# Gated-delta layer of a two-layer trunk: one decay matrix per unit, query products scaled after TensorE, the state's product set apart, the later modulation begun at the sixth unit

## The chip, the cores and the metric

The kernel runs on one core of one Trainium2 chip. Its engines work side by side and meet through semaphores: TensorE (PE in the profile, its weight loads PEld), VectorE (DVE), ScalarE (ACT), GpSimd (POOL) and the queue that starts the DMAs (SP). The metric is the time on the device of one execution, in microseconds (us). The kernel before takes 2041.61 us (median of 3 executions, 2041.05 to 2041.88).

## What is computed

Two layers on 1024 tokens of width 1024, all in float32. Layer A is a gated DeltaNet mixer, layer B a softmax attention with forget gates; only layer A is touched. In each layer the input is normalised and modulated by a shift, a scale and a gate that come from a conditioning vector (`cond @ ada_w[i]`). For layer A, per head and per chunk of tokens:

```python
g = jnp.cumsum(g, axis=-1)
decay = jnp.exp(jnp.where(lower, g[..., :, None] - g[..., None, :], -jnp.inf))
L = jnp.where(strict, jnp.einsum('bhncd,bhnsd->bhncs', kb, k) * decay, 0.0)
T = lax.linalg.triangular_solve(eye + L, ...)
u = T @ vb
w = T @ (kb * jnp.exp(g)[..., None])
attn = jnp.einsum('bhncd,bhnsd->bhncs', q, k) * decay
def step(state, inp):
    v_new = u_n - jnp.einsum('bhcd,bhde->bhce', w_n, state)
    o = (jnp.einsum('bhcd,bhde->bhce', q_n, state)
         + jnp.einsum('bhcs,bhse->bhce', a_n, v_new))
    state = state * gl_n[..., None, None] + jnp.einsum('bhcd,bhce->bhde', k_n, v_new)
    return state, o
```

Here q, k are normalised to length one, `kb`, `vb` are k and v times beta, `q_n` is q times exp(g), `k_n` is k times exp(g_last - g). There are 8 query/key heads and 16 value heads, so each key head serves two value heads.

## The kernel before

**Units.** Layer A is cut into 16 units: the sequence in two halves of 512 tokens (h = 0, 1), and in each half the 8 key heads (g = 0 to 7) with two value heads j each. The kernel uses chunks of 128 tokens (the result doesn't depend on the chunk), so a unit has 4 chunks. For each unit TensorE projects k, q, two times v and two gates z (`proj_tile`): 8 contraction steps of three matmuls with 512 columns each (high and low parts of the operands), evicted by `proj_conv` through ACT, three DVE steps of the short convolution and a tanh.

**A unit's steps**, each a Python generator:

- `decay` (L852) broadcasts the cumulated gates from DRAM into `gb` (128 x 1024), POOL masks it with an affine select (L861), and ACT takes exp with a bias, one instruction per head and chunk (L873). It runs twice a unit: `d1` (strictly lower, tokens on the partitions) for L, and `d2` (upper with diagonal, transposed) for attn.
- `prepk` (L878) brings k into token layout (`to_tokens`: 4 transposes, the squares on ACT, a copy to `ktok`, L919 and L923), forms 1/|k| with POOL's power (L888), the factors `un`, `wn`, `weg`, and L itself (`lm`) on DVE from the product k k^T in PSUM.
- `invert_blocks` inverts the 16 x 16 diagonal blocks: `lm`'s blocks go through DRAM into `lr` (one block per partition), 15 pairs of small DVE instructions (L1086, L1090) do the elimination, and the result comes back through DRAM into `r` (`rmat<-rb`). `invert_merge` then joins blocks to 32, 64 and 128 with small matmuls in banks "su" and "tr"; four DVE transposes (L1113) make `tm`, the transposed blocks, which its second group of matmuls needs.
- `prepv` (L926) brings q's squares and v into token layout (`vtok`, one copy of 128 x 512 per head, L923) and lets POOL scale v by `un` (L939, four instructions).
- `prep2` (L942) runs `decay` for d2, takes exp of `gb` on ACT (L949), multiplies q with it on POOL for each of the two heads (`qd`, L950), and forms `am` = (k q^T) times d2 on DVE (L958).
- `chain` (L962) is the recurrence, four chunks in order. Per chunk: PE k times state into bank "ch" (128 x 256); DVE `xp` (L978); PE r times `xp`; ACT copies it to `vn` (L991) and DVE scales it to `ve` (L992); then into bank "co", for each head, PE `qd` times state and `am` times `vn` accumulated, and at once `ktok` times `ve` (128 x 256); DVE updates the state (L1011); ACT takes the squares for the output norm and copies the output to `og` (L1017, L1020). Banks "ch" and "co" are single.
- `finish` (L1031) scales `og`, transposes it, multiplies with the z gate, splits it into high and low part (`ogh` on ACT, `ogl` on DVE) for both heads, and stores both with two DMAs of 512 KB.

**Other work.** `next_norm` normalises the second half's tokens during the first units. `ada_all` forms the later modulation (the gate of layer A, all of layer B) in 16 strips of 256 columns: 8 loads of 128 KB (`oraw`), 8 DVE instructions (L272, L274), a product with a vector of ones on PE, an eviction (L301) from a bank of the projections. It starts when the first gates are there. `out_proj_a` follows the projections.

**What sets the order.** PE's instructions stand in the order in which they are recorded. `Flow` keeps a list of generators with priorities and a clock of estimated PE time; each `yield n` makes its generator due n ns later, the first due one in priority order goes next, and the projections (priority 9) fill the rest. The numbers `Y_...` are such delays (how long a step waits for other engines' work before its next matmul is recorded), the numbers `R_...` say how long after the recording of an eviction its PSUM bank counts as free. They are estimates: if an engine is later than its number, PE waits, since it takes its instructions in order. The other engines' orders come from a scheduler with priorities; they too are fixed when the kernel is built, and each engine waits at its head instruction.

Of the kernel before, what the change touches and what calls it, by code (L numbers as in the profile page):

```python
# [8 lines left out]
F32 = mybir.dt.float32  # L9
F32R = mybir.dt.float32r  # L10
# [27 lines left out]
Y_PK = 1200  # L38
# [4 lines left out]
Y_P2 = 4000  # L43
# [8 lines left out]
Y_C2 = 2000  # L52
Y_F0 = 9000
Y_F1 = 800
Y_F2 = 2550
# [30 lines left out]
ADP = 2000  # L86
R_AD = 600
R_OA = 1150
# [95 lines left out]
def tile_trunk(  # L184
# [74 lines left out]
    def ada_strip(alloc, palloc, layer, col, width, wtag, atag, btag, ahead, pace):  # L259
# [38 lines left out]
        else:  # L298
# [3 lines left out]
            flow.free(ps, R_AD)  # L302
# [207 lines left out]
    with ExitStack() as sa:  # L510
# [34 lines left out]
        def start_norm():  # L545
            xsT = [at([P, HALF], n, b) for n, b in (("k", KQ), ("k", KQ), ("k", KQ), ("q", 2), ("q", 2))]
            xsT += [at([P, HALF], "ktok", 3) for _ in range(3)]
            for t in range(CPH):
                xt = at([P, D], *(("vtok", 3), ("qd", 2))[t // 2])
                nc.sync.dma_start(xt, x[t * P : (t + 1) * P, :])  # L550
                for d in norm_tile(xt, at([P, D], "ogt", 1), lambda k, p, t=t: nc.scalar.copy(
                    xsT[k][:, t * P : (t + 1) * P], p)):
                    flow.t += d
# [11 lines left out]
            for n in range(2):  # L565
                ps = banks[n]
                acc = at([P, D], "d2", 2)
# [43 lines left out]
        def norm_tile(xt, jk, evac):  # L611
            rs = rms_rows(xt, jk, at)
# [13 lines left out]
        def next_norm():  # L626
            yield from hold(lambda: done["kqv"] >= 2)
            for t in range(CPH):
                tok = CPH * P + t * P
                xt = at([P, D], "nx", 1)  # L630
                if t == 0:
                    nc.vector.tensor_copy(xt[:, 0:KT], ts[0]["gt"]["ngc"][:, 0, 0:KT])
                nc.sync.dma_start(xt, x[tok : tok + P, :])
                yield 4000
                hf = at([P, KT, P], "nh", 1)

                def evac(k, p):
                    nc.vector.tensor_scalar(
                        hf[:, k], p, gcol[0][:, k : k + 1], scol[0][:, k : k + 1],
                        op0=ALU.mult, op1=ALU.add,  # L640
                    )

                yield from norm_tile(xt, hf.rearrange("p k t -> p (k t)"), evac)
                yield 3000
                nc.sync.dma_start(
                    h1_d[:, :, t * P : (t + 1) * P].rearrange("k p t -> p k t"), hf
                )
# [12 lines left out]
        def gates(h, gt):  # L660
# [44 lines left out]
            nc.scalar.activation(ex, ex, AF.Exp)  # L705
            ngc = at([P, CPH, 16], "g_ngc", 2)
# [12 lines left out]
            gt.update(col=col, ex=ex, ngc=ngc, beta=beta, g_d=g_d)  # L719
# [54 lines left out]
        def proj_all():  # L774
            for i in range(2 * NG):
# [21 lines left out]
                yield from hold(lambda: done["prep2"] >= i - 1)  # L797
                t["q"] = qf = at([P, CPH, P], "q", 2)
# [53 lines left out]
        def decay(t, name):  # L852
# [6 lines left out]
            dv = at([P, 2 * CPH, P], name, 2)  # L859
            low = name == "d1"  # L860
            nc.gpsimd.affine_select(  # L861
                out=dv, in_=gb.rearrange("p j (c t) -> p (j c) t", t=P),
                compare_op=ALU.is_gt if low else ALU.is_ge, fill=BIG if low else -BIG, base=0,
                pattern=[[0, 2 * CPH], [-1 if low else 1, P]], channel_multiplier=1 if low else -1,
            )
            bias = t["gt"]["col" if low else "ngc"]
            yield Y_DG
            for j in range(2):
                for c in range(CPH):
# [4 lines left out]
                        dv[:, u], dv[:, u], AF.Exp, scale=-1.0 if low else 1.0, bias=bias[:, c, hd : hd + 1]  # L874
                    )
            return gb, dv

        def prepk(t):  # L878
            g, gt, kf = t["g"], t["gt"], t["k"]
            _, d1v = yield from decay(t, "d1")  # L880
            yield Y_PK
            t["ktok"] = ktok = at([P, CPH, P], "ktok", 3)
            t["ss"] = ss = at([P, 2, CPH], "gss", 3)
# [3 lines left out]
            nc.vector.tensor_scalar(rk, ss[:, 0], EPS, None, op0=ALU.add)  # L887
            nc.gpsimd.tensor_tensor(rk, rk, mhalf[:, 0:CPH], op=ALU.pow)  # L888
            rkb = bc(rk, 2, 2)
            t["un"] = un = at([P, CPH, 2], "un", 3)  # L890
            t["wn"] = wn = at([P, CPH, 2], "wn", 2)
            t["weg"] = weg = at([P, CPH, 2], "weg", 3)
# [967 lines left out]
```

## Time and profile before

| | us |
|---|---|
| median of 3 executions | 2041.61 |
| the profiled execution's own time | 2033.73 |
| its span | 2032.0 |
| PE busy in the span | 1846.4 |
| first to last projection matmul of layer A | about 45 to 1035 |
| output projection of layer A | about 1036 to 1281 |
| layer B | about 1281 to 2023 |

The profile is of one execution. A "wait" of PE is time in which PE had nothing running, put down to what released it. Two things are needed to read the PE rows. A matmul of plain float32 is two records, one of the split high/low type is one. And a record's length is modelled and overlaps the next record, so what a matmul costs is read from start to start, not from its length. The granted clock (PEclk) is 1.0 at full speed and 0.5 when throttled.

### The profile page before, as it was taken

The page shows a single profiled execution, that of the slowest core. Times are in us where ns is not written, and L with a number is a line of the kernel's source. Part 1 is how long each engine was busy: PE and PEld are TensorE (multiplying, and loading weights), DVE is VectorE, ACT ScalarE, POOL GpSimd, SP SyncE. Part 2 cuts the span into 40 slices and gives each one's busy share as a digit, 9 for nine tenths or more (in the row PEclk, how much of TensorE's full clock was granted, in tenths as well). Part 3 has the DMA queues.
Part 4 walks back from the last instruction along what each step waited for, and adds up shares of the span by engine and source line. Part 5 has one row for each costly group of instructions (what it writes and reads, how often), then busy time and mean ns, then how long its engine had stood idle before and what let it go on. Part 6 is the DMA issues. An engine that isn't in the chain of part 4 may idle for free. (4 is left out here: it accounts for less than half of the span.)

```text
span 2032.0 us, 36238 instructions
## 1 busy us (share of the span) xinstructions
PE 1846.4 (91%) x12940; PEld 1539.1 (76%) x12940; DVE 1375.5 (68%) x3319; ACT 1035.2 (51%) x2684; POOL 483.0 (24%) x518
## 2 busy tenths in 40 slices
PE   4878899998998989999989789999999999999898
PEld 3766677777776777777777567789889889889676
DVE  5788888787878566766656467456666666656764
ACT  4555466555545445555444344255655655655631
POOL 2140232221213021222101223331231231331222
PEclk6999899999999999999999899999999999999999
DMA  6686676766656455454469988020110220211523
GB/s 248 229 258 226 219 240 208 227 214 223 187 173 172 127 160 160 155 163 134 134 225 311 328 299 285 23 64 22 63 63 17 68 63 16 65 56 42 167 85 96
DMA packets 235781, 315.72 MB, mean 155 GB/s; under 512 B 103176, under 2 KB 155936, under 8 KB 235600
## 3 DMA queue, kind: packets, MB, share of 16 engines
q1 hardware_dynamic: 235600, 313.41, 47.6%
q8 instruction: 102, 1.67, 0.3%
q14 instruction: 79, 0.65, 0.1%
HBM read 231.67 MB, written 81.67 MB: 154 GB/s over the span
## 5 line engine op out<-in xcount | busy, mean ns | idle before, releaser
L129 PE MATMUL mm<-ht_h,whi 128*128 128x512 f32 x784 | 352.4, 450 | 7.2 <-DVE olo L301 5.6
L129 PE MATMUL mm<-ht_l,whi 128*128 128x512 f32 x784 | 317.5, 405 | 3.9 <-DVE ht_l L601 3.9
L129 PE MATMUL mm<-ht_h,wlo 128*128 128x512 f32 x784 | 318.0, 406 | 1.8 <-POOL wlo L328 1.8
L129 PE MATMUL mm<-whi,h_h 128*128 128x384 f32 x512 | 187.0, 365 | 0.9 <-DVE kn L1449 0.9
L129 PEld LDWEIGHTS mm<-ht_h,whi 128*128 128x128 f32 x784 | 154.6, 197 | 40.1 <-DVE olo L301 6.5
L129 PEld LDWEIGHTS mm<-ht_h,wlo 128*128 128x128 f32 x784 | 153.4, 196 | 37.8 <-POOL wlo L328 2.2
L129 PEld LDWEIGHTS mm<-ht_l,whi 128*128 128x128 f32 x784 | 155.0, 198 | 31.0 <-DVE ht_l L601 5.2
L764 DVE SCALAR_TENSOR_TENSOR cv_y<-cv_t,conv_h,cv_y 128x512 f32<-128x512 f32 x192 | 147.6, 769 | 43.0 <-ACT cv_y L756 40.8
L129 PE MATMUL mm<-whi,h_l 128*128 128x384 f32 x512 | 173.0, 338 | 0.0
L129 PE MATMUL mm<-wlo,h_h 128*128 128x384 f32 x512 | 172.7, 337 | 0.0
L1600 DVE TENSOR_TENSOR ptl<-pt,pth 128x512 fp32r<-128x512 f32 x192 | 106.3, 555 | 93.9 <-ACT pth L1599 92.2
L1599 ACT CAST pth<-pt 128x512 fp32r<-128x512 f32 x192 | 91.1, 476 | 140.0 <-PE pt L133 139.2
L1443 POOL TENSOR_TENSOR rs<-ss,mhalf 128x4 f32<-128x4 f32 x64 | 64.5, 1007 | 332.4 <-DVE ss L1441 326.7
L328 DVE TENSOR_TENSOR wlo<-ht_h,whi 128x512 fp32r<-128x512 f32 x124 | 91.1, 775 | 59.7 <-ACT whi L325 54.7
L1564 ACT ACTIVATE lg<-lg,mx 128x896 f32<-128x896 f32 (+7 forms) x128 | 99.5, 777 | 55.4 <-DVE mx L1556 49.7
L325 ACT CAST whi<-ht_h 128x512 fp32r<-128x512 f32 x124 | 70.7, 618 | 95.8 <-PE mm L129 35.3
L129 PE MATMUL mm<-h_h,whi 128*128 128x512 f32 x240 | 99.9, 416 | 0.7 <-DVE wlo L1699 0.3
L129 PEld LDWEIGHTS mm<-whi,h_h 128*128 128x128 f32 x512 | 97.8, 191 | 3.5 <-ACT v L1445 1.2
L129 PEld LDWEIGHTS mm<-wlo,h_h 128*128 128x128 f32 x512 | 97.4, 190 | 2.0
L133 PE MATMUL pt<-ident,lg 128*128 128x128 f32 (+1 forms) x584 | 95.6, 272 | 2.4 <-ACT lg L1564 2.4
L325 ACT CAST whi<-wlo 128x512 fp32r<-128x512 f32 (+1 forms) x108 | 62.5, 625 | 67.2 <-DMA wlo<-in_wa_c_dram 30.9
L129 PEld LDWEIGHTS mm<-whi,h_l 128*128 128x128 f32 x512 | 96.6, 189 | 0.0
(366 smaller groups left out, 4702.0 us busy)
## 6 DMA issues: line engine op xcount, KB each, us to landing
ht_h<-in_wa_o_dram SPq DMA_DIRECT2D x62, 512.0 KB
wc<-whi SPq DMA_DIRECT2D x45, 512.0 KB
wc<-wlo SPq DMA_DIRECT2D x45, 512.0 KB
wlo<-wc SPq DMA_DIRECT2D x45, 512.0 KB
whi<-wc SPq DMA_DIRECT2D x45, 512.0 KB
wlo<-in_wa_c_dram SPq DMA_DIRECT2D x35, 512.0 KB
oraw<-in_ada_w_dram SPq DMA_DIRECT2D x128, 128.0 KB
gb<-g_d SPq DMA_DIRECT2D x32, 512.0 KB
```

The costliest lines, as they stand in the source:

```text
L129: self.nc.tensor.matmul(out, lhsT, rhs, start=start, stop=stop)
L133: self.nc.tensor.transpose(out, src, ident)
L325: nc.scalar.copy(hi, src)
L328: (lo_eng or nc.gpsimd).tensor_tensor(lo, src, hi.bitcast(F32), op=ALU.subtract)
L764: nc.vector.scalar_tensor_tensor(y, raw[:, j : j + HALF], w[:, j : j + 1], y, op0=ALU.mult, op1=ALU.add)
L1443: nc.gpsimd.tensor_tensor(rs, ss, mhalf[:, 0:4], op=ALU.pow)
L1564: nc.scalar.activation(lg, lg, AF.Exp, scale=-1.0, bias=mx[:, hh : hh + 1], accum_out=sums[:, tt : tt + 1],)
L1599: nc.scalar.copy(ph_[:, cs], pp[:, cs])
L1600: nc.vector.tensor_tensor(pl_[:, cs], pp[:, cs], ph_[:, cs].bitcast(F32), op=ALU.subtract)
```

## The change

It touches layer A alone.

- **One decay matrix.** `d1` is no longer computed. `lm` is built from `d2`, so it holds the transposed L; the inversion's elimination and the merging matmuls are rewritten for that (operands swapped, same counts). The first group of the merging matmuls now reads the transposed blocks `tm`. A unit has one load of `gb`, one affine select and 8 exps in place of two, two and 16.
- **Scalings moved.** v is scaled by |k| while ACT takes it out of PSUM (two instructions of 128 x 256 per bank), where before POOL multiplied it. `vn` is scaled by beta/|k|^2 while ACT takes it out (two of 128 x 128 in place of one of 128 x 256). exp of `gb` on ACT and `qd` on POOL are gone.
- **Query product.** In place of `qd` times state in bank "co" per head, one product q times state (128 x 256) goes into bank "ch" right behind r times `xp`; ACT takes it out scaled by exp(g), two instructions (`qe`, L1023); DVE adds it to the output on the way out of "co" (`og`); the squares are then taken from `og`.
- **The state's product apart.** Between `am` times `vn` and `ktok` times `ve` stands a delay `Y_C3` = 1000. Other delays: `Y_C2` 2000 to 1700, `Y_PK` 1200 to 1000, `Y_P2` 4000 to 3000; bank "ch" counts as free 1000 ns later.
- **Later modulation.** `ada_all` starts when the sixth unit's k is recorded, and the bank of a gate strip counts as free 2500 instead of 600 ns after its eviction (`R_AS`).
- **Smaller ones.** q has three buffers; `next_norm` loads ahead into two buffers and stores by half tiles; `finish` works head by head with `ogt`, `ogh`, `ogl` of one head, single buffers, and four stores of 256 KB.

```diff
-Y_P2 = 4000
+Y_P2 = 3000
...
-Y_C2 = 2000
+Y_C2 = 1700
+Y_C3 = 1000
...
+AD0 = 5
 R_AD = 600
+R_AS = 2500
...
-            flow.free(ps, R_AD)
+            flow.free(ps, R_AS)
...
-                yield from hold(lambda: done["prep2"] >= i - 1)
-                t["q"] = qf = at([P, CPH, P], "q", 2)
+                t["q"] = qf = at([P, CPH, P], "q", KQ)
...
         def prepk(t):
-            _, d1v = yield from decay(t, "d1")
+            t["d2"] = yield from decay(t)
...
                     nc.vector.scalar_tensor_tensor(
-                        d1v[:, u], mq[:, c * P : (c + 1) * P], wn[:, c, j : j + 1], d1v[:, u],
+                        lm[:, u], mq[:, c * P : (c + 1) * P], wn[:, c, j : j + 1], t["d2"][:, u],
...
+                    nc.scalar.activation(
+                        vtok[:, c].rearrange("p j f -> p (j f)"), tr[:, o : o + 2 * P], AF.Copy,
+                        scale=t["irk"][:, c : c + 1],
+                    )
...
-            for c in range(CPH):
-                nc.gpsimd.tensor_tensor(vtok[:, c], vtok[:, c], bc(t["un"][:, c], 2, P), op=ALU.mult)
...
-            gb, d2 = yield from decay(t, "d2")
...
-                nc.scalar.activation(gb[:, j], gb[:, j], AF.Exp)
-                nc.gpsimd.tensor_tensor(
-                    qd[:, j], qf, gb[:, j].rearrange("p (c t) -> p c t", t=P), op=ALU.mult
-                )
...
-                nc.scalar.copy(vn, p1[:, 256:512])
+                for j in range(2):
+                    nc.scalar.activation(
+                        vn[:, j * P : (j + 1) * P], p1[:, 256 + j * P : 256 + (j + 1) * P], AF.Copy,
+                        scale=wn[:, c, j : j + 1],
+                    )
...
-                flow.free(p1, R_C)
+                if not first:
+                    mm(p1[:, 0:256], qf[:, c], st)
+                    qe = at([P, 2 * P], "qe", 2)
+                    for j in range(2):
+                        sl = slice(j * P, (j + 1) * P)
+                        nc.scalar.activation(
+                            qe[:, sl], p1[:, sl], AF.Copy, scale=ex[:, 1, c, 2 * g + j : 2 * g + j + 1]
+                        )
+                flow.free(p1, R_C + 1000)
                 yield Y_C1
                 p2 = yield from pst("co", 1)
                 for j in range(2):
                     sl = slice(j * P, (j + 1) * P)
-                    if not first:
-                        mm(p2[:, sl], qd[:, j, c], st[:, sl], start=True, stop=False)
-                    mm(p2[:, sl], am[:, j, c], vn[:, sl], start=first, stop=True)
+                    mm(p2[:, sl], am[:, j, c], vn[:, sl])
+                yield Y_C3
                 mm(p2[:, 256:512], ktok[:, c], ve.rearrange("p j f -> p (j f)"))
...
+                    nc.vector.tensor_tensor(oc, p2[:, 0:256], qe, op=ALU.add)
...
-                nc.scalar.copy(og[:, c].rearrange("p j f -> p (j f)"), p2[:, 0:256])
...
+                ogt = at([P, HALF], "ogt", 1)
...
+                ogh, ogl = at([P, HALF], "ogh", 1, F32R), at([P, HALF], "ogl", 1, F32R)
+                split(ogh, ogl, ogt, lo_eng=nc.vector)
+                yield Y_F2
+                for v, d in ((ogh, og_d), (ogl, ogl_d)):
+                    nc.sync.dma_start(d[2 * g + j, :, h * HALF : (h + 1) * HALF], v.bitcast(F32))
...
-                        pbk[b][o : o + 16, us], lm[sls[b], u, o : o + 16], r[sls[b], u, o + 16 : o + 32],
+                    mm(pbk[b][sls[b], us], lm[h16, u, sls[b]], tms[b][0:16, u, 0:16], start=True, stop=True)
...
         def ada_all():
-            yield from hold(lambda: done["gates"] == 1)
+            yield from hold(lambda: done["kp"] >= AD0 + 1)
```

Three places show how the instructions move. First ACT's order before, at the first unit: `sqt` are the squares of transposed k (L919), d_731 is the first unit's `d1`, `ktok` and `vtok` the copies that free PSUM bank "tr".

```order
L919 ACTIVATE sqt,gss<-tr 128x128
L873 ACTIVATE d_731<-d_731,g_gc 128x128 x8
L919 ACTIVATE sqt,gss<-tr 128x128 x3
L923 COPY ktok<-tr 128x512
L768 ACTIVATE cv_t<-cv_y 128x512
L919 ACTIVATE sqt,gss<-tr 128x128 x2
L923 COPY vtok<-tr 128x4x128
```

ACT's order now, at the same place (d_734 is the one decay matrix `d2`):

```order
L935 ACTIVATE sqt,gss<-tr 128x128 x4
L939 COPY ktok<-tr 128x512
L935 ACTIVATE sqt,gss<-tr 128x128 x4
L787 ACTIVATE cv_t<-cv_y 128x512
L889 ACTIVATE d_734<-d_734,g_ngc 128x128 x8
L956 ACTIVATE vtok<-tr,irk 128x256 x4
```

The eight exps have moved from ahead of three of k's squares and the `ktok` copy to behind them and behind q's squares.

Second PE's order before, in one chunk of the chain of the second unit (state_140 is its state, d_1214 its `am`, mm the projections that fill):

```order
L133 MATMUL tr<-ident,og 128x128 x4
L129 MATMUL co<-state_140,qd 128x128
L129 MATMUL co<-vn,d_1214 128x128
L129 MATMUL co<-state_140,qd 128x128
L129 MATMUL co<-vn,d_1214 128x128
L129 MATMUL co<-ve,ktok 128x256
```

PE's order now, in the same chunk:

```order
L132 MATMUL ch<-xp,rmat_129 128x128 x2
L132 MATMUL ch<-state_140,q 128x256
L136 MATMUL tr<-ident,og 128x128 x4
...
L132 MATMUL co<-vn,d_832 128x128 x2
L132 MATMUL mm<-ht_h,whi 128x512
L132 MATMUL mm<-ht_l,whi 128x512
L132 MATMUL mm<-ht_h,wlo 128x512
L132 MATMUL mm<-ht_h,whi 128x512
L132 MATMUL mm<-ht_l,whi 128x512
L132 MATMUL mm<-ht_h,wlo 128x512
L136 MATMUL tr<-ident,og 128x128 x4
L132 MATMUL co<-ve,ktok 128x256
```

The product with `ve` stood directly behind the ones with `vn`; now six projection matmuls stand between. Of the 64 chunks 36 have six there, 18 have three and 10 none; before, none had any.

Third ACT's order before, with what each waits for, at the second unit's `finish` (`ogh` are its two heads' high parts, DMAHW a DMA's semaphore):

```order
L325 CAST ogh<-ogt 128x512 [waits DMAHW6_49,DVE_49]
L1167 ACTIVATE rmat_128<-su 32x8x32 [waits PE_49]
L1169 ACTIVATE rmat_128<-su 32x8x32 [waits PE_49]
L923 COPY vtok<-tr 128x4x128 [waits PE_49]
L325 CAST ogh<-ogt 128x512 [waits DVE_49]
```

ACT's order now, at the same unit's `finish`:

```order
L328 CAST ogh<-ogt 128x512 [waits DVE_49]
L328 CAST whi<-wlo 128x512
L829 ACTIVATE cv_t<-mm 128x512 [waits PE_49]
L830 COPY zg<-mm 128x512
L1205 COPY pq<-su 64x512 [waits PE_49]
L328 CAST ogh<-ogt 128x512 [waits DMAHW5_49,DVE_49,Activation_49]
L328 CAST whi<-wlo 128x512 [waits DMAHW6_49,DMAHW4_49,PE_49]
```

The second cast now waits for the store of the first head's half, issued a few instructions before; it waited for DVE alone.

182 lines of the change are left out of this document (95 added, 87 removed).

## The prediction, made before the result was known

> **What bounds the kernel now.** I read the page first, for the busiest engine.
>
> ```profile
> PE 1846.4 (91%) x12940; PEld 1539.1 (76%) x12940; DVE 1375.5 (68%) x3319; ACT 1035.2 (51%) x2684; POOL 483.0 (24%) x518
> ```
>
> PE is busy for 91% of the span, no other engine for more than 68%. So time goes only where PE works less or waits less. Next the busy time by stages, cut at layer A's start phase, the rest of its projections, and its output projection (the columns are PE, PEld, DVE, ACT, POOL, then the granted clock).
>
> ```profile
> 45.00:200.00 155.00, 127.01 (x981) 100.12 (x982) 127.34 (x308) 85.15 (x215) 32.95 (x46) 0.89 0.71 231
> 200.00:1035.00 835.00, 760.44 (x6580) 619.95 (x6579) 619.54 (x1579) 440.89 (x1347) 180.12 (x230) 0.96 0.57 179
> 1035.00:1281.00 246.00, 217.43 (x1170) 170.64 (x1169) 149.73 (x260) 104.59 (x218) 54.04 (x36) 0.96 0.86 292
> ```
>
> The change lies in the first two rows. There PE stands still for 28.0 and 74.6 us, 102.6 in all, and at clocks of 0.89 and 0.96 it loses another 0.11 x 155 + 0.04 x 835 = 50 us of clock. The third stage and layer B keep their work, so I leave them as they are. Who holds PE up is in the list of waits, first for 45 to 200 us:
>
> ```profile
> PE su L129 <- DMA rmat<-rb: 9.5, 1, 9.5
> PE tr L133 <- ACT ktok L923: 6.0, 1, 6.0
> PE mm L129 <- DVE ht_l L601: 3.9, 2, 3.4
> PE mm L129 <- DVE olo L301: 3.2, 2, 2.4
> ```
>
> and for 200 to 1035 us (total, number, longest):
>
> ```profile
> PE co L129 <- DVE ve L992: 19.0, 14, 2.3
> PE tr L133 <- ACT vtok L923: 15.4, 4, 7.0
> PE ch L129 <- DVE xp L978: 10.7, 6, 2.6
> PE co L129 <- ACT vn L991: 7.1, 7, 2.8
> PE tr L133 <- ACT sqt L919: 2.9, 2, 2.4
> PE mm L129 <- DVE olo L301: 2.4, 1, 2.4
> PE su L129 <- ACT pp L1153: 2.3, 2, 1.2
> PE mm L129 <- ACT cv_y L756: 2.2, 1, 2.2
> ```
>
> The first list is the first unit, which has little to hide behind; the second is the chain and evictions that come late.
>
> **PE's own work: no gain.** The query product changes from two 128-wide products a chunk to one 256-wide, in the 56 chunks that have a state. PE's rows in order of start:
>
> ```profile
> 712.93 0.39 PE L129 MATMUL co<-state,qd 128*128 128x128 f32 x2
> 713.15 0.39 PE L129 MATMUL co<-vn,d 128*128 128x128 f32 x2
> 713.38 0.60 PE L129 MATMUL co<-ve,ktok 128*128 128x256 f32 x2
> 713.62 0.58 PE L129 MATMUL mm<-ht_h,whi 128*128 128x512 f32 x1
> 714.04 0.39 PE L129 MATMUL mm<-ht_l,whi 128*128 128x512 f32 x1
> 714.27 0.40 PE L129 MATMUL mm<-ht_h,wlo 128*128 128x512 f32 x1
> ```
>
> From start to start a 128-wide product takes 713.15 - 712.93 = 0.22 us. A 256-wide one and a projection matmul together take 714.04 - 713.38 = 0.66, and a projection matmul alone 714.27 - 714.04 = 0.23, so the 256-wide one takes 0.43. Two narrow ones 0.44, one wide 0.43: 56 x 0.01 = 0.6 us, which I leave out. The other products keep their number and width, and so do the merging matmuls (operands swapped only). The Trainium skill speaks for more: "TensorE: Matmul & The Clock Gate", Back-to-back issue gap, gives 81 ns a matmul at 128 columns against 131 at 512 in a stream of weight loads and matmuls, far less than in proportion. By an estimate from that page (98 ns at 256 columns, two passes each) the 56 chunks would gain 56 x 2 x (162 - 98) ns = 7 us; the rows above show proportion, so the sum goes by them.
>
> **What leaves the other engines.** POOL's groups:
>
> ```profile
> L939 POOL TENSOR_TENSOR vtok<-vtok,un 128x256 f32<-128x256 f32 x64 | 44.8, 730 | 78.6 <-ACT vtok L923 71.3 <-DVE xi L1090 7.4
> L950 POOL TENSOR_TENSOR qd<-q,gb 128x512 f32<-128x512 f32 x32 | 43.1, 1368 | 27.4 <-ACT gb L949 19.1 <-DVE q L771 4.8 <-DVE rk L887 3.5
> L861 POOL TENSOR_SCALAR_AFFINE_SELECT d<-gb 128x1024 f32<-128x1024 f32 x32 | 36.1, 1129 | 118.1 <-PE co L129 52.5 <-DMA gb<-g_d 39.5 <-PE su L129 17.6
> ```
>
> The first two go and half of the third: 44.8 + 43.1 + 18.0 = 106 us. That is worth something to DVE, as rows of both engines in time order show: beside a POOL select a 30-wide step of the inversion took 1.01 us, without POOL the same step takes 0.18.
>
> ```profile
> 725.04 1.09 POOL L861 TENSOR_SCALAR_AFFINE_SELECT d<-gb 128x1024 f32<-128x1024 f32 x1
> 725.16 1.01 DVE L1090 TENSOR_TENSOR xi<-xi,xtmp 128x30 f32<-128x30 f32 x1
> ...
> 954.73 0.18 DVE L1090 TENSOR_TENSOR xi<-xi,xtmp 128x30 f32<-128x30 f32 x1
> ```
>
> So up to 0.83 us of DVE is lost in 1.09 us of POOL; over 106 us that is between 0 (no DVE instruction of that kind beside it) and 80 us. I take 45, as DVE is busy for 74 to 82% of these stages and not all it does reads SBUF twice. DVE gets the new output sum, one instruction a chunk of the shape of `ve`:
>
> ```profile
> L992 DVE TENSOR_TENSOR ve<-ch,g_ex 128x256 f32<-128x256 f32 x64 | 26.8, 419 | 10.8 <-ACT vn L991 10.3
> L274 DVE SCALAR_TENSOR_TENSOR ohi<-oraw,cond,ohi 128x256 f32<-128x256 f32 x112 | 65.5, 584 | 14.2 <-DMA oraw<-in_ada_w_dram 13.4
> ```
>
> 56 x 0.419 = 23 us; on balance DVE loses some 22. The second row is the later modulation: what of its 65.5 us ran in the first five units leaves them, where DVE is at 82%, and comes back where it is at 74%. The 16 loads of `gb` that go (512 KB each) I cost at nothing, since the DMA engines are at 0.57 to 0.71 there (the column before GB/s).
>
> ACT:
>
> ```profile
> L873 ACT ACTIVATE d<-d,g_gc 128x128 f32<-128x128 f32 x128 | 39.2, 389 | 22.6 <-POOL d L861 13.7 <-POOL cv_t L759 8.9
> ...
> L991 ACT COPY vn<-ch 128x256 f32<-128x256 f32 x64 | 24.0, 374 | 36.8 <-PE ch L129 36.6
> ...
> L949 ACT ACTIVATE gb<-gb 128x512 f32<-128x512 f32 x32 | 18.4, 618 | 0.0
> ```
>
> and one of its rows in time, eight exps of 128 x 128 in a run, with the PE row that was waiting behind them:
>
> ```profile
> 97.19 2.45 ACT L873 ACTIVATE d<-d,g_gc 128x128 f32<-128x128 f32 x8 [0.57 <-POOL d L861]
> ```
>
> ```profile
> 101.22 1.11 PE L133 MATMUL tr<-ident,vt 128*128 128x128 f32 x4 [5.99 <-ACT ktok L923]
> ```
>
> The exps leave (-39.2 - 18.4 = -57.6 us). A 128 x 128 activation with a scale costs 2.45 / 8 = 0.31 us in a run. `vn` becomes two of them for one of 0.374: +0.24 a chunk, 64 x 0.24 = +15. `qe` is two a chunk: 56 x 0.61 = +34. The copy of `og` goes (priced as `vn`'s shape, 56 x 0.374 = -21); v's evictions in twice as many pieces cost 0 to 12, I take 5. ACT: -25 us in all, but +0.24 us on each chunk's way from r times `xp` to the output. A rule of the skill speaks against the change here: "ScalarE: Activation LUTs", What ACT_TABLE_LOAD costs, adds about 93 ns for every per-partition operand, such as these scales. By that page the split `vn` would be an estimated 0.28 us later instead of 0.24; no row before shows this very instruction.
>
> **The sum, in waits of PE.**
>
> 1. First unit. The 6.0 us on `ktok`: the exps stood ahead of k's squares in ACT's queue and themselves waited for POOL; they now stand behind. What is late next is the squares of q, eight short ACT instructions: 4 of the 6.0 go (0 to 5.5). The 9.5 us on `rmat`: the inversion's small DVE steps ran between modulation steps and beside POOL; without both, and with lb's blocks ready earlier, I take 8.5 of 9.5 (3 to 9.5), PE's place for the merging is the same. The 3.2 us on `olo`: no strip there any more, all of it. Together -16.
> 2. Strips later on: the 2.4 us on `olo` and 2.2 on `cv_y` are projections waiting for a strip's bank; the longer hold lets PE do something else first: -4 (-4.6 to 0).
> 3. Chain. The 19.0 us on `ve` are 14 waits, 1.36 each. Now six projection matmuls (1.4 us) fill 36 of 64 chunks, three (0.7) another 18: about 0.8 to 0.9 of each wait goes, -12 (-17 to 0; filling moves no work, it only moves it ahead). `xp`: DVE is freer, -3 of 10.7 (0 to -6). `vn`: 0.24 later each, 7 waits: +2 (0 to +15, all 64 chunks). Net -13.
> 4. Evictions. 15.4 on `vtok` and 2.9 on `sqt`: ACT has 25 us less, no exps of `d1` in the way, but v's copy now needs |k|: -6 (-12 to +4).
> 5. Clock. 50 us of clock were lost beside 102.6 us of standing still. If 39 us of waits go, in proportion 19 us of clock; part of that lies in the waits themselves, where it costs nothing: -6 (-17 to 0).
> 6. New waits. The merging's first matmuls need the DVE transposes:
>
> ```profile
> L1113 DVE STREAM_TRANSPOSE tmat<-rmat 32x256 f32<-32x256 f32 x64 | 27.9, 435 | 20.3 <-DMA rmat<-rb 18.8
> ```
>
> Four take 1.74 us a unit, so 0 to 28 us; they follow a DMA on which PE, after the first unit, waited less than the list's smallest row in any one line, so they are mostly done in time: +4. The second `ogh` cast waits for a store: POOL waited 39.5 us on 32 loads of `gb` (row above), 1.2 each, so 31 casts cost ACT 0 to 38 us; behind it stand weight casts and `vn`; ACT is at 53%, a tenth reaches PE: +4. Strips beside the later units: 0 to +5, I take 2. Bank "ch" held until `qe` is out: 0 to +8, I take 2. Together +12.
>
> Sum: -16 - 4 - 13 - 6 - 6 + 12 = -33. The profiled execution took 2033.73 us (span 2032.0 and 1.7 around it), 7.9 less than the median 2041.61. I let that difference stand: 2000.7 in a profile like this one, 2041.6 - 33 = **2008.6** as the median. The query product, the finer stores of the normalised half and the third buffer of q I cost at nothing: PE's list has no wait for the latter two (uncovered, the stores would show as a wait on the loads of the second half).
>
> **Rivals.**
>
> *Start only.* Terms 1 and 2 hold, but filling in front of `ve` only moves the wait: the next chunk's state comes 1.4 us later, and PE meets it at `ch`. Against it: that list is sorted, and it has no wait on the state at 2.2 us or above, so the state comes early enough to give some time away. -16 - 4 + 12 = -8: 2034.
>
> *ACT becomes the bound (slower).* Per chunk `vn` is 0.24 and `qe` 0.61 us of new ACT work before bank "ch" is free and the output leaves. If PE meets them at every chunk, that is 64 x 0.85 = 54 us against terms 1 to 5 (-45) and the rest of term 6 (+10): +19, 2061. It decides from 41 of 64 chunks on (35 / 0.85); now 7 meet `vn`. Against: ACT is at 53% in this stage and gets less to do.
>
> *More.* PE is read by its lengths: the `qd` products were 224 records of 0.28 us, the new ones 112 of 0.39, some 20 us less, or the page's 7; or the waits of the second list go nearly whole with their clock. Either gives another 15 to 30: 1978 to 1993. The start-to-start times speak against the first.
>
> *No change.* The gain in waits is eaten by as many new ones, since the orders of DVE and ACT are all redrawn: 2041.
>
> **How the numbers follow.** My forecast has 0.55, start only 0.20, more 0.12, slower 0.08, no change 0.05. A measurement of this kernel can tell about 0.2% (4 us) from no change. Faster: 0.55 + 0.12 + three quarters of start only = 0.82; same: 0.05 + 0.03 = 0.08; slower: 0.08 + 0.02 = 0.10. The forecast's own bounds are some 16 us either way (the first unit's 8, the chain's 10, term 6's 8, not all at once). The range takes in start only to its upper end and half of more: 1980 to 2036.
>
> **What would show it.** Right: the wait on `rmat` in the first unit under 3 us, `ktok` under 2; `ve` under 8 us in total; PE's mean clock in 200 to 1035 above 0.96; POOL some 106 and ACT some 25 us less, the inversion's small steps at 0.2 us; PE's product rows at 0.43 us. Wrong: waits on `vn`, `qe`'s bank or `ogh` of 20 us or more, PE first at the merging waiting for L1113's transposes in many units, or a layer A that is shorter only before 200 us.

## The result, and the profile after

Slower: 2113.72 us (median of 4 executions, 2100.45 to 2117.61) against 2041.74 before on the same chip, a ratio of 1.034 (95% interval 1.029 to 1.039). The forecast was 2008.6, with a range of 1980 to 2036. The profiled execution took 2111.84 us, 78.1 more than the one before (2033.73), and its page shows where. Below are the busy line and the row of PE with the most idle time in front of it (line, operation, count, then busy time and mean ns, then the idle time before it and who ended it):

```profile
span 2110.1 us, 35950 instructions
...
PE 1875.9 (89%) x12828; PEld 1555.0 (74%) x12828; DVE 1348.6 (64%) x3394; ACT 1038.7 (49%) x2676; POOL 366.6 (17%) x406
...
L132 PE MATMUL ch<-state,q 128*128 128x256 f32 x112 | 44.5, 483 | 104.9 <-DVE ve L1014 104.9
```

The new query product, priced at nothing in the forecast, has 104.9 us of standing still in front of it, all ended by `ve`. It doesn't use `ve`. The list of PE's waits in the second stage, which the forecast's second list answers to (total, number, longest):

```profile
PE ch L132 <- DVE ve L1014: 90.8, 49, 3.5
PE ch L132 <- DVE state L1040: 8.0, 8, 1.7
PE su L132 <- DVE tmat L1168: 3.7, 2, 3.0
PE ch L132 <- DVE xp L996: 3.5, 5, 1.2
```

Before, `ve` held PE 14 times, 19.0 us in this stage; now in every one of the 56 chunks with a state (49 here, 7 in the two stages beside it), 1.87 us each. The rows of one chunk in time show how (start, length, engine):

```profile
449.89 0.60 PE L132 MATMUL ch<-xp,rmat 128*128 128x128 f32 x4
...
450.69 0.63 ACT L787 ACTIVATE cv_t<-cv_y 128x512 f32<-128x512 f32 x1 [0.42 <-DVE cv_y L783]
451.35 0.62 ACT L1010 ACTIVATE vn<-ch,wn 128x128 f32<-128x128 f32 x2
451.36 0.69 DVE L790 SCALAR_TENSOR_TENSOR q<-cv_t,cv_y 128x512 f32<-128x512 f32 x1 [0.76 <-ACT cv_t L787]
452.01 0.42 DVE L1014 TENSOR_TENSOR ve<-ch,wex 128x256 f32<-128x256 f32 x1
452.48 0.30 PEld L132 LDWEIGHTS ch<-state,q 128*128 128x128 f32 x2 [2.18 <-DVE ve L1014]
452.48 0.70 PE L132 MATMUL ch<-state,q 128*128 128x256 f32 x2 [1.99 <-DVE ve L1014]
...
452.83 0.58 PE L132 MATMUL mm<-ht_h,whi 128*128 128x512 f32 x1
```

PSUM is the memory into which PE writes its products, and "ch" is one bank of it, 512 columns wide. r times `xp` ends at 450.49 in columns 256 to 511 of this bank. ACT finishes something else, reads them for `vn` until 451.97, then DVE reads them for `ve` until 452.43; only then, at 452.48, PE starts the query product into columns 0 to 255. In all 56 chunks it starts 0.05 to 0.06 us after the end of `ve`. The projection matmuls that were to cover the read-out stand behind the product, since the change records it ahead of the fill `Y_C1`. The Trainium skill has the rule ("PSUM — Partial Sum Buffer", section "PSUM bank collisions raise a hardware error"): two engines may not touch the same bank and the same 32 partitions at once, disjoint columns included and ACT beside DVE too, and the compiler orders such instructions. The trace agrees in both: 56 of 56 products wait for the reader of the other half, and `ve`, which needs nothing of `vn`, waits for it. What a collision would do, which the page tells as well, no run here can show.

The stages, with the forecast's columns and the new stage ends:

```profile
45.00:200.00 155.00, 130.24 (x992) 104.20 (x993) 107.31 (x270) 85.01 (x209) 13.75 (x33) 0.88 0.62 200
200.00:1101.00 901.00, 778.30 (x6469) 626.88 (x6469) 611.24 (x1684) 441.09 (x1332) 83.37 (x131) 0.95 0.52 162
1101.00:1362.00 261.00, 224.70 (x1159) 174.86 (x1159) 153.58 (x268) 108.16 (x230) 54.29 (x36) 0.94 0.81 275
```

The projections end 66 us later, layer A's output projection 81 us later (six of the waits, 10.8 us, lie in that stage), and layer B keeps its length. In the whole span PE stood still for 2110.1 - 1875.9 = 234.2 us (before 185.6, +48.6), and its busy time grew by 29.5 us with fewer instructions: the granted clock is 0.95 instead of 0.96 in the long stage and 0.94 instead of 0.96 in the last one, and a product that starts out of a wait is longer (both in the last section). 48.6 + 29.5 = 78.1. The waits on `ve` and `vn` alone grew by 104.9 - 26.6 = 78 us (before: 19.5 and 7.1), so the other waits together fell by some 30.

### The profile page after: what moved, and what is told of

It is laid out like the page before. It is cut to its first block, busy times and chain, and to the rows that moved or that the text cites. A ratio compares the mean times of both kernels' runs of the same rounds, so it can differ in the third digit from the quotient of the medians.

```text
span 2110.1 us, 35950 instructions
## 1 busy us (share of the span) xinstructions
PE 1875.9 (89%) x12828; PEld 1555.0 (74%) x12828; DVE 1348.6 (64%) x3394; ACT 1038.7 (49%) x2676; POOL 366.6 (17%) x406
## 5 line engine op out<-in xcount | busy, mean ns | idle before, releaser
L132 PE MATMUL mm<-ht_h,whi 128*128 128x512 f32 x784 | 360.6, 460 | 3.3 <-ACT whi L328 2.0
L331 DVE TENSOR_TENSOR wlo<-ht_h,whi 128x512 fp32r<-128x512 f32 x124 | 95.6, 813 | 66.0 <-ACT whi L328 59.2
L132 PE MATMUL ch<-state,q 128*128 128x256 f32 x112 | 44.5, 483 | 104.9 <-DVE ve L1014 104.9
L132 PEld LDWEIGHTS ch<-state,q 128*128 128x128 f32 x112 | 18.4, 207 | 115.7 <-DVE ve L1014 115.7
```

Source lines behind the costliest of these rows:

```text
L132: self.nc.tensor.matmul(out, lhsT, rhs, start=start, stop=stop)
L331: (lo_eng or nc.gpsimd).tensor_tensor(lo, src, hi.bitcast(F32), op=ALU.subtract)
```

## The experiments

**Does the wait cost the loss, and does the bank make the wait?** Four kernels, E1 to E4, answer this. E1 moves the product with its scalings behind the fill:

```diff
-                if not first:
-                    mm(p1[:, 0:256], qf[:, c], st)
...
-                flow.free(p1, R_C + 1000)
                 yield Y_C1
+                if not first:
+                    mm(p1[:, 0:256], qf[:, c], st)
...
+                flow.free(p1, R_C + 1000)
```

> The changed kernel with the query product, its two scalings and the release of bank ch moved behind the fill Y_C1, so that on average some nine other PE matmuls (1.95 us at 0.23 us each) stand between r times xp and the product; nothing else differs. Theory A (PE stands still because the product writes bank ch while vn and ve are still being read out of it): the 56 waits of 104.9 us on ve are 1.87 us each, so nearly all are covered; the wait on ve at the product falls below 20 us and the time by 70 to 100 us, to 2015 to 2045. Theory B (the added scalings make ACT the bound, or hold bank ch): the same instructions are still there, the wait moves to the vn product or to the next k product, and the time stays above 2085. Theory C (the loss comes from other parts, such as the finer stores or the later strips): no change, 2105 to 2120.

E2 leaves its place and changes its bank (`pst("tr", 2)` takes one of the two banks "tr"):

```diff
-                    mm(p1[:, 0:256], qf[:, c], st)
+                    ps = yield from pst("tr", 2)
+                    mm(ps[:, 0:256], qf[:, c], st)
...
-                            qe[:, sl], p1[:, sl], AF.Copy, scale=ex[:, 1, c, 2 * g + j : 2 * g + j + 1]
+                            qe[:, sl], ps[:, sl], AF.Copy, scale=ex[:, 1, c, 2 * g + j : 2 * g + j + 1]
+                    flow.free(ps, R_T)
```

> The changed kernel with the query product in the same place, right behind r times xp, but written to a bank of ring tr instead of the free half of ch. Theory A: the product has no reader of its bank to wait for and runs at once; the wait on ve at the product is gone, what is left of it shows behind the fill at the vn and ve products (under 30 us in all, 19.0 + 7.1 before the change); time 2005 to 2045. Theory A' (the place alone decides: PE would meet the same delay anywhere right behind r times xp): 2100 to 2120. Theory B (ACT): above 2085.

E3 puts the query part alone into the kernel before:

```diff
-            t["qd"] = qd = at([P, 2, CPH, P], "qd", 2)
-            for j in range(2):
...
+                if not first:
+                    mm(p1[:, 0:256], qf[:, c], st)
+                    qe = at([P, 2 * P], "qe", 2)
...
-                        mm(p2[:, sl], qd[:, j, c], st[:, sl], start=True, stop=False)
-                    mm(p2[:, sl], am[:, j, c], vn[:, sl], start=first, stop=True)
+                    mm(p2[:, sl], am[:, j, c], vn[:, sl])
...
+                    nc.vector.tensor_tensor(oc, p2[:, 0:256], qe, op=ALU.add)
```

> The kernel before with the query part alone: no exps of gb and no POOL product qd, the product of q and the state in the free half of ch right behind r times xp, two ACT scalings, the sum with the output on DVE, and a third buffer of q. One decay matrix per unit, the other scalings, the finish, the merging and the modulation stay as before. Theory A: the whole loss lies here; vn is one copy instead of two (0.25 us sooner), so each wait is about 1.6 instead of 1.87 us, 56 x 1.6 = 90 us, less some 20 of the old waits on ve and vn that go: 2041 + 70 = 2110 (2090 to 2130). Theory C (other parts lose): 2030 to 2060.

E4 is a dose between the changed kernel and E1:

```diff
+                yield 700
                 if not first:
                     mm(p1[:, 0:256], qf[:, c], st)
...
-                yield Y_C1
+                yield Y_C1 - 700
```

> The changed kernel with 0.7 us of the fill Y_C1 moved ahead of the query product, which by the order puts some six matmuls (1.24 us on average) between r times xp and the product. A dose between the changed kernel and the product behind the whole fill. Theory A: each of the 56 waits is shorter by what the fill covers, about 1.2 of 1.87 us: wait on ve 25 to 50 us, time 2040 to 2075. Theory B or C: 2100 or more.

Measured (ratios to the kernel before on the same chip, 95% interval; waits and sums from the profiled executions):

| kernel | ratio | wait on `ve` at the product | PE standing still | PE busy |
|---|---|---|---|---|
| before | 1 | none | 185.6 | 1846.4 |
| E2, other bank | 0.988 (0.986 to 0.990) | 0 | 164.8 | 1843.7 |
| E1, behind the fill | 0.998 (0.996 to 1.000) | 32.8 | 181.9 | 1850.4 |
| E4, dose | 1.008 (1.007 to 1.010) | 57.0 | 200.2 | 1849.6 |
| changed kernel | 1.034 (1.029 to 1.039) | 104.9 | 234.2 | 1875.9 |
| E3, query part alone | 1.056 (1.053 to 1.059) | 111.7 | 267.5 | 1888.1 |

The product's rows of E2, E1, E4 and E3:

```profile
L132 PE MATMUL tr<-state,q 128*128 128x256 f32 x112 | 33.8, 383 | 1.2 <-ACT vtok L956 1.1
```
```profile
L132 PE MATMUL ch<-state,q 128*128 128x256 f32 x112 | 38.0, 422 | 33.3 <-DVE ve L1014 32.8
```
```profile
L132 PE MATMUL ch<-state,q 128*128 128x256 f32 x112 | 40.3, 443 | 57.2 <-DVE ve L1014 57.0
```
```profile
L129 PE MATMUL ch<-state,q 128*128 128x256 f32 x112 | 46.8, 505 | 111.7 <-DVE ve L984 111.7
```

In the same place but in another bank, the product has no wait on `ve`, and the kernel is faster than before. E2's rows of one chunk show it, beside those of the changed kernel above:

```profile
450.31 0.61 PE L132 MATMUL ch<-xp,rmat 128*128 128x128 f32 x4
450.76 0.60 PE L132 MATMUL tr<-state,q 128*128 128x256 f32 x2
451.41 0.64 ACT L1010 ACTIVATE vn<-ch,wn 128x128 f32<-128x128 f32 x2
...
452.40 0.42 DVE L1014 TENSOR_TENSOR ve<-ch,wex 128x256 f32<-128x256 f32 x1
```

In 49 of the 56 chunks E2's product stands directly behind r times `xp`, and there it starts without any wait, each time before `ve` is done. In the other seven PE's order has 3 to 82 other records between the two, since the product is recorded only when a bank "tr" counts as free. So it is the shared bank, not the place. A PSUM tile is a whole bank in this kernel, so the runs can't tell a wait by bank from a wait by tile.

The wait follows the dose, and the time the wait. Both waits are larger than was expected (E1 32.8 against under 20, E4 57.0 against 25 to 50, with 42 of 56 products still waiting); both times are as expected (2034.55 and 2053.02 us). E3 shows that the whole loss, and more, lies in the query part; its expectation had the mechanism and too small a size (2150.55 us, expected up to 2130), since the old waits on `ve` and `vn` at "co" went down to 11.0 us only and those on `xp` rose to 14.9. What the rest of the change is worth is the difference to the changed kernel: 1.056 - 1.034, some 2.2%, or 1.2% by E2. Behind the whole fill 18 products still wait, up to 4.0 us (E1): the read-out stands behind other work on ACT and DVE, as in the chunk shown, and this fill doesn't cover all of that.

**Is ACT the bound, as the rival said?** E8 issues each of the two scalings twice:

```diff
-                        nc.scalar.activation(
+                        for _ in range(2):
+                            nc.scalar.activation(
```

> The changed kernel with the query product in ring tr and each of its two scalings issued twice, the second a repetition of the first: 112 more ACT instructions of 0.31 us, 35 us of ACT, with the output unchanged. Theory A (ACT is not the bound and its added work hides): within 0.004 of the run with single scalings, ratio 0.986 to 0.992. Theory B (ACT's added scalings bound the chunk): 56 x 0.62 = 35 us longer, or a good part of it: ratio 0.998 to 1.006.

E7 records the product still earlier, so that its scalings stand ahead of `vn` on ACT:

```diff
                     mm(p1[:, 0:256], kf[:, c], st)
...
+                    ps = yield from pst("tr", 2)
+                    mm(ps[:, 0:256], qf[:, c], st)
...
                     yield Y_C0
...
-                if not first:
-                    mm(p1[:, 0:256], qf[:, c], st)
...
```

> The query product in ring tr, recorded right behind the product of k and the state, ahead of r times xp. Theory A: it has no reader to wait for, fills 0.43 us of the time that xp takes on DVE, and its two scalings leave ACT ahead of vn instead of behind: the same as right behind r times xp or up to 8 us less, ratio 0.984 to 0.989. If the scalings in front of vn hold up vn (ACT's order decides): the wait on vn rises from 4.8 to 15 us or more, ratio 0.990 to 0.996.

The page of E8:

```profile
PE 1841.2 (92%) x12828; PEld 1526.3 (76%) x12828; DVE 1346.5 (67%) x3394; ACT 1066.5 (53%) x2788; POOL 369.2 (18%) x406
```

ACT is 34.5 us busier than in E2 (1032.0), and the ratio is 0.986 (0.984 to 0.989): the added work costs nothing that shows. The amount of ACT's work is not the bound. E7 gives 0.986 (0.983 to 0.989); its waits on `vn` rise from 4.8 to 7.3 us, less than was named for the case that ACT's order decides.

**The forecast's smaller terms.** E5 undoes the later start of the modulation on top of E2 (the longer hold `R_AS` stays), E6 the fill `Y_C3` on top of E2, E9 both:

```diff
-            yield from hold(lambda: done["kp"] >= AD0 + 1)
+            yield from hold(lambda: done["gates"] == 1)
...
```
```diff
-                yield Y_C3
```

> The changed kernel with the query product in ring tr (as in the run before, ratio 0.988), and the later modulation undone: the strips start with the gates of the first half again. Theory D (the forecast's terms 1 and 2 hold: the early strips delay the first unit's inversion and hold PE up): the gain of about 20 us that the first 294 projection matmuls show is lost again and stays lost, time 10 to 20 us above the run before: 2022 to 2032, ratio 0.994 to 1.000. Theory E (the strips only move: what the start gains, the later units give back): ratio within 0.003 of 0.988, or below it.

> The changed kernel with the query product in ring tr and the state's product recorded straight behind the product of the decay matrix and vn again (no fill Y_C3 between). Theory F (the forecast's third term: the fill hides what PE waited for ve): the wait on ve at co rises from 5.8 back to 15 to 25 us and the time by 8 to 15 us, ratio 0.992 to 0.996. Theory G (the fill only moves the wait on to the next chunk's state): the wait on ve rises, that on the state (10.1 us at ch) falls by as much, ratio within 0.003 of 0.988.

> The changed kernel with three edits: the query product in ring tr, the strips from the gates of the first half on again, and no fill Y_C3. The three one by one gave ratios of 0.988 (first alone), 0.980 (first and second) and 0.980 (first and third). Theory K (the later modulation and the fill each cost about 16 us in themselves): the gains add, 0.988 - 0.008 - 0.008 = 0.972, 0.968 to 0.976, some 1980 us. Theory L (each edit only redraws the order of the engines, and both runs drew well): 0.978 to 0.988.

E10 puts the fill alone into the kernel before:

```diff
-Y_C2 = 2000
+Y_C2 = 1700
+Y_C3 = 1000
...
+                yield Y_C3
                 mm(p2[:, 256:512], ktok[:, c], ve.rearrange("p j f -> p (j f)"))
```

> The kernel before with one part of the change alone: the fill Y_C3 between the output's and the state's products, and Y_C2 1.7 instead of 2.0 us, as in the changed kernel. Theory F (the forecast's third term): the 19.0 us of waits on ve fall to about 7, ratio 0.992 to 0.996. Theory K (the fill itself costs, since it moves the state, which the next chunk waits for, 1 us later): the wait on ve falls, those on the state and on xp rise, ratio 1.002 to 1.010. Neither: 1.000.

E11 the later strips:

```diff
...
+AD0 = 5
...
+R_AS = 2500
...
-            flow.free(ps, R_AD)
+            flow.free(ps, R_AS)
...
-            yield from hold(lambda: done["gates"] == 1)
+            yield from hold(lambda: done["kp"] >= AD0 + 1)
...
```

> The kernel before with another part alone: the strips from the sixth unit on, with the longer hold of their banks (2.5 instead of 0.6 us). Theory D (the forecast's terms 1 and 2): the waits on olo (3.2 and 2.4 us) and a part of that on rmat (9.5) go and stay gone, ratio 0.993 to 0.997. Theory K (the strips cost more beside the later units, where PE has little slack, than at the start, where it waits anyway): projection 294 is some 20 us earlier, the last one is not, ratio 1.002 to 1.010.

E12 is E6 with the strips in between:

```diff
-AD0 = 5
+AD0 = 2
```

> The changed kernel with the query product in ring tr, no fill Y_C3, and the strips from the third unit on instead of the sixth. If the start's gain of 20 us and the later units' gain can be had together: 0.966 to 0.972. Theory K (the earlier the strips, the better, for what they take later): between 0.972 and 0.980. Theory L: 0.978 to 0.988.

E6 gives 0.980 (0.978 to 0.982), E5 0.980 (0.977 to 0.982), but both edits together 0.990 (0.988 to 0.992), and E12 0.980 (0.978 to 0.982). So the gains don't add. E6 and E9 lie outside both of the ranges that were named for each. E10 gives 1.006 (1.004 to 1.008), E11 1.006 (1.004 to 1.008). That raised the question how much any edit moves the time by redrawing the order. E13 to E18 change one spacing by 0.05 us and nothing else: E13 and E14 in E2, E15 in E9, E16 in the kernel before, E17 in E5, E18 in E6. In all but E14 it is

```diff
-Y_PS = 3000
+Y_PS = 3050
```

and in E14

```diff
-Y_PT = 650
+Y_PT = 700
```

> The changed kernel with the query product in ring tr, and one spacing of the order 0.05 us longer (Y_PS 3.05 instead of 3.00 us), which means nothing by itself but redraws the order in some two thirds of PE's rows. Theory L (what a redrawn order costs or saves is of the size of the forecast's small terms): the ratio differs from 0.988 by 0.004 or more, up or down. Theory K (the order's chance is small, so the 16 us of the later strips and of the fill are their own): 0.985 to 0.991.

> The same kernel with another meaningless edit (Y_PT 0.70 instead of 0.65 us), which redraws about a quarter of PE's rows. Theory L: 0.978 to 0.998, not within 0.003 of both the run with Y_PS changed and 0.988. Theory K: 0.985 to 0.991.

> The version with all three edits (product in ring tr, early strips, no fill; 0.990) with Y_PS 3.05. Theory L: differs from 0.990 by 0.004 or more, most likely down to 0.978 to 0.986, since 0.990 was the worst draw of four kernels with this product. Theory K: 0.987 to 0.993.

> The kernel before with Y_PS 3.05 alone. Theory L, for a kernel whose spacings were chosen by their times: slower by 0.3 to 1 per cent, 1.003 to 1.010, so that the 0.6 per cent of the fill alone and of the later strips alone may be the redrawn order and not the part. Theory K: 0.998 to 1.002.

> Product in ring tr and early strips, with the fill (0.9795), and Y_PS 3.05. The four meaningless redraws moved the time by 0.1 to 0.3 per cent. If 0.9795 is a property of this combination: 0.977 to 0.983. If it was a lucky draw: 0.984 or more.

> Product in ring tr, late strips and no fill (0.980), with Y_PS 3.05. A property of the combination: 0.977 to 0.983; a lucky draw: 0.984 or more.

The kernel before went to 1.002 (1.001 to 1.004). The others, all with the product in ring "tr" (half of an interval is 0.002):

| | with the fill `Y_C3` | without it |
|---|---|---|
| strips from the sixth unit | 0.988 (E2), 0.985 (E13), 0.985 (E14) | 0.980 (E6), 0.981 (E18) |
| strips from the first gates | 0.980 (E5), 0.992 (E17) | 0.990 (E9), 0.989 (E15) |

Three of the four fields repeat within 0.3%; in the fourth 0.05 us of one spacing cost 1.2%. It is not the chip: E6 and E18, measured beside E5 and E17 on the same two chips, agree within 0.2%. So E5 was a lucky order, and my additive reading of it was wrong. What holds over the two or three orders of each field: with the later strips (upper row) the fill costs some 0.5%, and without the fill (right column) the later strips gain some 0.9%. In the lower row and the left column E5 and E17 lie too far apart to say. E11, where the later strips cost 0.6% in the kernel before, is one order, and stays open: projection matmul 294 (of 2352, counted from 0) starts there 9 us earlier than before, the last one 17 us later.

What the fill does to PE's waits is seen in E10, again one order. PE's waits in the chain, in the second stage:

```profile
PE ch L130 <- DVE state L1013: 11.0, 9, 3.2
PE ch L130 <- DVE xp L979: 8.7, 6, 3.9
...
PE co L130 <- ACT vn L992: 5.9, 6, 2.5
PE co L130 <- DVE ve L993: 5.0, 6, 2.1
```

`ve` fell from 19.0 to 5.0, as the forecast had it, and the state rose from 1.3 to 11.0 (12.1 with another row): the state's product now comes about 1 us later, and the next chunk meets it. E6, without the fill, has the reverse only in part: `ve` 9.7 instead of 5.8 in E2, the state 11.5 instead of 12.6. These two are 2.8 us worse together, while the time is some 16 us better. So the later state is not shown to be what the fill costs; where the 0.5% lies stays open.

The best version that held in a second order (E18) is E6: the change with the product in another bank and without the fill, 1996.81 us, 2% below the kernel before.

## Why the prediction was wrong

**The step that failed** is one sentence: "The query product, the finer stores of the normalised half and the third buffer of q I cost at nothing". PE's own work was right (no more time for the product itself: 33.8 us for 112 records in E2, where the old ones took 44.7 for 224); that the product adds a wait, and which work stands behind it, wasn't asked. Term 6 lists new waits, and bank "ch" only as "held until `qe` is out: 0 to +8, I take 2", that is, for what comes after the product; what it must wait for before it was left out. The hint stood in a row that the prediction quotes: `ve` before the change had 10.3 us of idle time ended by `vn`, though it needs nothing of `vn`. Two readers of one bank were already kept apart; a writer into its other half had to be expected to queue behind both. With that, the row prices were there: two ACT instructions of 0.31 and `ve` of 0.42 make 1.04 us at the least, 56 times, 58 us, more than the whole forecast gain, and no fill in between. Measured were 1.87 us each, 104.9 in all, and none under 1.17: on average 0.27 us pass before ACT begins `vn`, and 0.50 between its end and the start of `ve`, in which DVE still has other work.

**The other steps**, measured on E2, the change without that wait (profiled: 2010.2 us, 23.5 below before; -33 forecast):

| term | forecast | E2 against before |
|---|---|---|
| 1. first unit | -16 | `ktok` 6.0 to 2.7, `olo` 3.2 to 0, `rmat` 9.5 to `tmat` 8.6: -7 |
| 2. later strips, `olo` and `cv_y` 4.6 | -4 | `olo` 2.4 to 0, `cv_y` 2.2 to 1.0: -4; the effect on the time depends on the fill (above) |
| 3. chain: `ve`, `xp`, `vn` | -13 | `ve` -13, `xp` -7, `vn` -2, but the state +11: -11; in time the fill costs 0.5% (above) |
| 4. evictions `vtok`, `sqt` | -6 | 15.4 to 3.7, 2.9 to 3.8: -11 |
| 5. clock | -6 | PE busy -3, at 0.97 instead of 0.96 |
| 6. new waits | +12 | merging on its transposes (`tmat`) +12 after the first unit, the product on its new bank 1.2 |

E2's waits in 45 to 200 us and in 200 to 1020 us, from which this is read:

```profile
PE su L132 <- DVE tmat L1141: 8.6, 2, 7.8
...
PE tr L136 <- ACT ktok L939: 2.7, 1, 2.7
```
```profile
PE ch L132 <- DVE state L1042: 10.1, 9, 3.4
PE su L132 <- DVE tmat L1195: 7.1, 4, 2.3
PE co L132 <- DVE ve L1014: 5.8, 5, 1.6
PE co L132 <- ACT vn L1010: 4.8, 5, 2.4
PE su L132 <- DVE tmat L1141: 4.7, 2, 4.5
...
PE tr L136 <- ACT sqt L935: 3.8, 2, 2.1
PE tr L136 <- ACT vtok L956: 3.7, 4, 1.8
PE ch L132 <- DVE xp L996: 3.4, 3, 2.2
PE ch L132 <- DVE state L1040: 2.5, 2, 2.0
```

The term of the first unit failed at "PE's place for the merging is the same": in the order it is, in time it isn't. The inverted blocks let the merging start 8.7 us earlier (145.8 instead of 154.5), but PE, with the other waits and the strips out of its way, comes to it 7.1 us earlier (138.0 instead of 145.1) and stands there 7.8 instead of 9.5 us. The time wasn't lost: projection 294 starts at 137.1 instead of 157.0. Later 4 us of this go again: the last projection is 15.9 us earlier, not 20. In term 3 the filling (-12) came out the other way: some 10 us slower in time. The rival *Start only*, by which it only moves the wait to the state, fits E10's waits (`ve` 14.0 less, the state 10.8 more), though E6 leaves open what the time goes to.

**The other engines.** POOL has 483.0 - 366.6 = 116 us less (106 forecast). `vn` and `qe` came as priced:

```profile
L1010 ACT ACTIVATE vn<-ch,wn 128x128 f32<-128x128 f32 x128 | 40.1, 364 | 42.2 <-PE ch L132 42.0
...
L1023 ACT ACTIVATE qe<-ch,g_ex 128x128 f32<-128x128 f32 x112 | 35.0, 364 | 72.6 <-PE ch L132 72.4
...
L1014 DVE TENSOR_TENSOR ve<-ch,wex 128x256 f32<-128x256 f32 x64 | 26.8, 419 | 20.0 <-ACT vn L1010 19.5
```

40.1 - 24.0 = +16 and +35 (+15 and +34 forecast). The split makes `vn` 0.25 us longer per chunk (16.1 / 64), and the forecast took 0.24 from its rows. The estimate from the Trainium skill ("ScalarE: Activation LUTs", What ACT_TABLE_LOAD costs) was 0.28; the measured 0.25 lies between the two. On the profile's page ACT lost nothing (1038.7 against 1035.2; -25 forecast). Summed over its rows it lost 15 (1154.5 to 1139.3); the profile's page has the smaller times, as it counts time in which two records overlap once. The squares of the output (now 39.6, before 35.2) and v's scaled evictions (26.7, before 18.7, of which 5 were forecast) are where the rows came out above the forecast. DVE lost 27 (22 forecast): the 480 small steps of the inversion took 89.1 us instead of 120.1. The last row above shows ACT and DVE kept apart again: 19.5 us in which DVE waits for `vn` before `ve`. The rival "ACT becomes the bound" had the right sign, but too small a size (2061) and the wrong reason: "ch" is not held long by ACT's new work; PE is shut out of it.

"A layer A that is shorter only before 200 us" and waits of 20 us or more on `qe`'s bank were named as signs that the prediction is wrong. The first came: in the changed kernel projection matmul 294 is 20 us earlier than before, 735 already 2 us later. The bank was the right one, and the wait stood on its other side.

## What to carry to other kernels

Before a matmul is moved into a free half of a PSUM bank, list who still reads the other half at that point of the order: here it waited for all of them, and everything recorded behind it on PE waited too. An instruction priced at nothing can cost more than all others if it is recorded ahead of the fill that was to cover a read-out; another bank, at the same place, gave back 4.6% of the time here. And where a written-out order sets the time, one run of a variant says little below half a per cent to one per cent: repeat it with an edit that means nothing, before a term is credited with it.

## What was not expected of the hardware

The waits cost more than their length. PE's busy time for the same 12828 records goes from 1843.7 us in E2 to 1875.9 in the changed kernel. The traces' records of the granted clock tell where most of it lies. The clock stands at half for 147.9 us of E2's span and for 201.7 of the changed kernel's, and PE is busy for 106.1 and 163.1 us of these. From start to start a projection matmul takes 0.23 us at full and 0.43 at half clock (medians in both kernels). So the 57 us more at half clock make an estimated 26 of the 32 us. Much of the rest is the product itself: its first record, behind the wait, is 483 ns long in 46 of 56 chunks where E2 has 382 in 49, and 56 times 0.10 is 6 us.

Why the clock is at half more often isn't shown. It doesn't simply follow the waits: the mean granted clock of the profiled executions is 0.963 in E2, 0.959 in E1, 0.963 in E4 (57.0 us of waits), and only then 0.952 in the changed kernel and 0.941 in E3.

A change of 0.05 us in one estimated spacing moved the time by 0.1 to 0.3% in five kernels (E13 to E16, E18), which is hardly clear of the noise, and by 1.2% in a sixth (E17), which is.
